# Last bank in pieces of 384 and 128 columns, its last store split by partitions over both hardware queues

## The chip, the cores and the metric

One core of a Trainium2 chip. The metric is the device time of one execution in microseconds (us), of which several are taken; all runs with rounds were in the fast state, with a mean granted TensorE clock of 0.996 to 1.0; the three single looks (e6, e10, e11) are of unknown state. "Before" is the kernel as it was, "the change" the kernel with the diff below.

Since everything happens in the last six microseconds, I use one more measure, the **tail**: from the start of the add of output row block k = 6 (the last instruction chain that the diff leaves alone) to the end of the span. It is read from one profiled execution and does not contain the few tenths by which whole executions differ from one another earlier on.

## The reference

```python
def reference(input, grad_output):          # (16, 512, 1024), (16, 512, 768), float32
    return np.einsum('bmk,bmn->kn', input, grad_output)      # (1024, 768)
```

A matrix product that contracts over 8192 rows, in 64 slices of 128. The kernel rounds the inputs to bf16.

## The kernel before

512 of the 768 output columns are computed in the "wide" form: for each of eight blocks k of 128 output rows, a slice of the input is the weight and 512 columns of grad_output are streamed. Most slices are summed early, in parts, into `acc` in SBUF. The end of the kernel is the last 14 slices (50 to 63) of each of the eight blocks: 14 matmuls into one PSUM bank (where TensorE sums), an add to `acc` on VectorE, a store to HBM (the chip's main memory). Stores are issued by SyncE or by ACT (ScalarE), each with a DMA queue of its own. The last block is cut into three column pieces, so that the last add and the last store are small. Four stores of the other 256 columns (`turned`) stand before that in the program, on the ACT queue; in time the last of them is issued at 162.82 us, just before the store of k = 4.

```python
    rows_of = out.rearrange("(b r) n -> r b n", r=SQ)
    for a in range(P // SQ):
        c = NA + a * NT * SQ
        nc.scalar.dma_start(
            out=rows_of[:, :, c : c + NT * SQ],
            in_=turned[a * SQ : (a + 1) * SQ].rearrange("p b r t -> p b (r t)"),
        )

    for k in range(KS):                                   # KS = 8, NA = 512, NB = 256, P = 128
        slices = range(parts["A" if k < KS // 2 else "B"].done, S)          # 50 .. 63
        pieces = [(0, NA)] if k < KS - 1 else [(0, 256), (256, 384), (384, NA)]
        for c0, c1 in pieces:
            name = free.pop(0)
            bank = psum.tile([P, NA], f32, name=name)[:, 0 : c1 - c0]
            for s in slices:
                wide_mm(bank, k, s, s == slices[0], s == slices[-1], c0, c1)
            add_out(acc[:, k, c0:c1], bank)               # VectorE: acc += bank
            free.append(name)
            W = NB if k < 6 else c1 - c0                  # columns per store
            for c in range(c0, c1, W):
                nc.sync.dma_start(out=OUT[:, k, c : c + W], in_=acc[:, k, c : c + W])
```

## Time and profile before

| | before |
|---|---|
| time, median of the first 3 runs (of the 6 that the change is compared with) | 176.0 us (175.99) |
| span of the profiled execution | 174.3 us |
| TensorE busy | 97% of the span |
| last add ends | 171.79 us into the span |
| last store: issue to landing | 1.54 us |
| last landing to the end of the span ("closing") | 0.92 us |
| tail | 5.86 us |

The prediction shows most of the profile lines on which this rests (in these views DVE is VectorE; SPq and ACTq are the sequencers of SyncE and ACT, which issue the stores). The add of k = 6:

```profile
168.41 0.69 DVE L118 TENSOR_TENSOR acc<-bank,acc 128x512 f32<-128x512 f32 x1 [2.33 <-PE bank L127]
```

The finer times are start times of single records of the trace: an add's start and duration, an issue's start, the last increment of a store's completion semaphore (its "landing"). They read as a relay: matmuls of a piece, add, issue by a queue, bytes in motion, landing, closing. From the last add on nothing else runs beside it, so whatever one link costs the time pays in full.

### The profile page before, as it was taken

How to read it: one execution, taken by the hardware profiler on the slowest of the kernel's cores; microseconds unless marked ns; L12 is line 12 of the kernel's file. 1: busy time of each engine (PE TensorE's matmuls, PEld its weight loads, DVE VectorE, ACT ScalarE, POOL GpSimd, SP SyncE). 2: the span in 40 equal slices, each digit the busy share in tenths (PEclk: the TensorE clock that was granted, in tenths of full speed). 3: DMA queues.
4: the chain of work that ended last, by engine and by line, in shares of the span. 5: the costliest groups of instructions: out<-in, count | busy, mean ns of one | idle time of the engine just before them, and what ended most of it. 6: DMA issues, size and time to landing. Idle time of an engine off the chain costs nothing.

```text
span 174.3 us, 2013 instructions
## 1 busy us (share of the span) xinstructions
PE 169.9 (97%) x793; PEld 78.4 (45%) x808; DVE 61.3 (35%) x103; ACT 6.2 (4%) x12; POOL 66.7 (38%) x129
## 2 busy tenths in 40 slices
PE   8999999999999999999999999999999999999993
PEld 3444444444444444444444444444444444444463
DVE  0655582883940039300000662200560003931122
ACT  2640000000000000000000000000000000000000
POOL 7444434444444444444444444444274200000000
PEclk9999999999999999999999999999999999999999
DMA  5999999999999999999999999999999990085623
GB/s 192 276 208 209 207 209 208 208 208 209 207 208 209 207 208 210 207 209 209 206 209 208 208 210 207 207 209 208 207 209 209 207 202 11 0 190 160 170 86 120
DMA packets 25048, 33.35 MB, mean 191 GB/s; under 512 B 6480, under 2 KB 16592, under 8 KB 25040
## 3 DMA queue, kind: packets, MB, share of 16 engines
q0 software_dynamic: 18000, 28.65, 89.9%
q10 hardware_dynamic: 4448, 2.10, 4.7%
q1 hardware_dynamic: 2592, 2.49, 4.2%
q8 instruction: 6, 0.10, 0.2%
q14 instruction: 2, 0.02, 0.0%
HBM read 58.72 MB, written 3.15 MB: 355 GB/s over the span
## 4 chain that ended last, share of the span: by engine, by line
PE 97%; issue 0%; DVE 0%
PE bank L127 63%; PE bank L134 32%; PE bank L81 3%; DVE acc L118 0%
## 5 line engine op out<-in xcount | busy, mean ns | idle before, releaser
L127 PE MATMUL bank<-gt,xt 128*128 128x512 bf16 (+2 forms) x515 | 108.3, 367 | 0.5
L127 PEld LDWEIGHTS <-xt 128*128 128x128 bf16 x524 | 50.2, 98 | 57.2
L118 DVE TENSOR_TENSOR acc<-bank,acc 128x512 f32<-128x512 f32 (+2 forms) x62 | 37.9, 667 | 73.4 <-PE bank L127 72.9
L134 PE MATMUL bank<-xt,gt 128*128 128x512 bf16 x242 | 54.8, 379 | 0.3
L97 POOL DMA_DIRECT2D xt<-in_input_dram x62 | 33.1, 533 | 38.7 <-DMA xt<-in_input_dram 36.5
L92 POOL DMA_DIRECT2D gt<-in_grad_output_dram x63 | 33.8, 536 | 31.2 <-DMA gt<-in_grad_output_dram 24.9
L134 PEld LDWEIGHTS <-gt 128*128 128x128 bf16 x252 | 24.6, 98 | 29.7
L118 DVE TENSOR_TENSOR acct<-bank,acct 128x512 f32<-128x512 f32 x24 | 15.7, 682 | 30.0 <-PE bank L134 29.9
L81 PE MATMUL bank<-const-bfloat16-1.0 128*128 128x512 bf16 (+1 forms) x12 | 4.6, 574 | 0.8 <-PEq L263 0.8
L81 PEld LDWEIGHTS <-const-bfloat16-1.0 128*128 128x128 bf16 x12 | 1.6, 140 | 3.5 <-issue 3.5
L122 DVE COPY acc<-bank 128x512 f32<-128x512 f32 x4 | 2.7, 687 | 1.0 <-PE bank L127 1.0
L180 DVE STREAM_TRANSPOSE turned<-acct 128x512 f32<-128x512 f32 x4 | 2.9, 715 | 0.1
L127 PEld LDWEIGHTS <-x 128*128 128x128 bf16 x16 | 1.6, 98 | 1.9 <-DVE x L107 0.2
L107 DVE CAST g<-gf 128x256 bf16<-128x256 f32 x2 | 0.6, 290 | 4.7 <-DMA gf<-in_grad_output_dram 4.7
L124 ACT COPY acc<-bank 128x512 f32<-128x512 f32 x4 | 2.1, 589 | 1.3 <-PE bank L127 1.3
L127 PE MATMUL bank<-gt,x 128*128 128x512 bf16 x8 | 2.1, 379 | 0.0
L127 PE MATMUL bank<-g,x 128*128 128x512 bf16 x8 | 2.0, 398 | 0.0
L122 DVE COPY acct<-bank 128x512 f32<-128x512 f32 x2 | 1.3, 686 | 1.3 <-PE bank L134 1.3
L107 ACT CAST x<-xf 128x256 bf16<-128x256 f32 x4 | 1.4, 409 | 0.0
L107 ACT ACT_TABLE_LOAD x1 | 1.3, 1283 | 1.7 <-PEq L263 1.7
L124 ACT COPY acct<-bank 128x512 f32<-128x512 f32 x2 | 1.1, 588 | 1.5 <-PE bank L134 1.5
L107 DVE CAST x<-xf 128x256 bf16<-128x256 f32 (+1 forms) x5 | 1.0, 260 | 0.0
(8 smaller groups left out, 3.3 us busy)
## 6 DMA issues: line engine op xcount, KB each, us to landing
xt<-in_input_dram POOLq DMA_DIRECT2D x62, 256.0 KB, 8.5
gt<-in_grad_output_dram POOLq DMA_DIRECT2D x63, 192.0 KB, 8.5
out_dram<-acc SPq DMA_DIRECT2D x13, 128.0 KB, 2.7
xf<-in_input_dram ACTq DMA_DIRECT2D x2, 512.0 KB, 5.1
out_dram<-turned ACTq DMA_DIRECT2D x4, 256.0 KB, 3.4
gf<-in_grad_output_dram SPq DMA_DIRECT2D x1, 256.0 KB, 3.9
out_dram<-acc SPq DMA_DIRECT2D x1, 256.0 KB, 2.0
gf<-in_grad_output_dram SPq DMA_DIRECT2D x1, 128.0 KB, 4.7
```

The source lines that it names most:

```text
L81: nc.tensor.matmul(wps[:, 0:cols], ones, nc.const_aps.tensor(1.0, (P, cols), bf16), start=True, stop=True,)
L92: nc.gpsimd.dma_start(out=gt, in_=G[s * P : (s + 1) * P, :])
L97: nc.gpsimd.dma_start(out=xs[s], in_=X[s * P : (s + 1) * P, :])
L107: copy(out=dst[:, c0:c1], in_=src[:, c0:c1])
L118: nc.vector.tensor_add(out=dst, in0=src, in1=dst)
L122: nc.vector.tensor_copy(out=dst, in_=src)
L124: nc.scalar.copy(out=dst, in_=src)
L127: nc.tensor.matmul(bank, xs[s][:, k * P : (k + 1) * P], gwide[s][:, c0:c1], start=start, stop=stop)
L134: nc.tensor.matmul(bank, gnarrow[s].rearrange("p (r t) -> p t r", t=NT)[:, t], xs[s][:, h * NA : (h + 1) * NA], start=start, stop=stop,)
L180: nc.vector.transpose(out=turned[:, h * hb : (h + 1) * hb, :, t], in_=dst.rearrange("p (b r) -> p b r", r=SQ),)
```

## The change

Its intent: fewer pieces, so that TensorE ends a little earlier, and the last store in two halves of 64 partitions issued at once by both hardware queues, so that each has half of the rows to issue.

```diff
-        pieces = [(0, NA)] if k < KS - 1 else [(0, 256), (256, 384), (384, NA)]
+        pieces = [(0, NA)] if k < KS - 1 else [(0, 384), (384, NA)]
...
-            W = NB if k < 6 else c1 - c0
+            W = NB if k < KS - 2 else c1 - c0
+            if c1 == NA and k == KS - 1:
+
+                for eng, p0 in ((nc.scalar, 0), (nc.sync, P // 2)):
+                    eng.dma_start(
+                        out=OUT[p0 : p0 + P // 2, k, c0:c1], in_=acc[p0 : p0 + P // 2, k, c0:c1]
+                    )
+                continue
             for c in range(c0, c1, W):
                 nc.sync.dma_start(out=OUT[:, k, c : c + W], in_=acc[:, k, c : c + W])
```

The second hunk is no change of behaviour (KS - 2 is 6).

## The prediction

> **What bounds the kernel now.** I read the page's chain first, then the engine totals, to learn which engine sets the end.
>
> ```profile
> PE 169.9 (97%) x793; PEld 78.4 (45%) x808; DVE 61.3 (35%) x103; ACT 6.2 (4%) x12; POOL 66.7 (38%) x129
> ## 4 chain that ended last, share of the span: by engine, by line
> PE 97%; issue 0%; DVE 0%
> PE bank L127 63%; PE bank L134 32%; PE bank L81 3%; DVE acc L118 0%
> ```
>
> The chain is TensorE's own row of matmuls for 97% of the span. Nothing that the diff touches lies before the last of eight output rows (k = 7), so only the last few microseconds can change. The timeline of that stretch comes next (start, duration, engine, line, operation).
>
> ```profile
> 169.13 3.02 SPq L248 DMA_DIRECT2D out_dram<-acc  x4
> 169.94 0.42 DVE L118 TENSOR_TENSOR acc<-bank,acc 128x256 f32<-128x256 f32 x1 [0.84 <-PE bank L127]
> 170.72 0.29 DVE L118 TENSOR_TENSOR acc<-bank,acc 128x128 f32<-128x128 f32 x1 [0.36 <-PE bank L127]
> 171.50 0.29 DVE L118 TENSOR_TENSOR acc<-bank,acc 128x128 f32<-128x128 f32 x1 [0.49 <-PE bank L127]
> ```
>
> Each add starts when the fourteen matmuls of its piece are done, so the distances between add starts are the lengths of the pieces: k = 6 ended at 168.41 (the add before these in the same view), the 256-column piece took 169.94 - 168.41 = 1.53 us, each 128-column piece 0.78 us. The last add ends at 171.79, and the span at 174.3: 2.5 us with no compute at all. I looked into these with the stretch table (stretch, length, five engines, clock, DMA share, GB/s), cut where DMA activity starts and stops:
>
> ```profile
> 171.20:171.70 0.50, 0.26 (x5) 0.09 (x2) 0.20 (x1) 0.00 (x0) 0.00 (x0) 1.00 0.77 262
> 171.85:172.20 0.35, 0.00 (x0) 0.00 (x0) 0.00 (x0) 0.00 (x0) 0.00 (x0) 1.00 0.64 187
> 172.60:173.00 0.40, 0.00 (x0) 0.00 (x0) 0.00 (x0) 0.00 (x0) 0.00 (x0) 1.00 0.57 164
> 173.00:174.30 1.30, 0.00 (x0) 0.00 (x0) 0.00 (x0) 0.00 (x0) 0.00 (x0) 1.00 0.00 0
> ```
>
> The first three rows are the stores of the 256-, 128- and 128-column pieces (262 x 0.50 = 131 KB; 187 x 0.35 and 164 x 0.40 = 65 KB each). Before and between them the DMA engines are idle. The last store alone reads:
>
> ```profile
> L248 SPq DMA_DIRECT2D out_dram<-acc x1: 333/333/333, 171.8 to 171.8; - x1
> DMA to landing us min/median/max: 1.5/1.5/1.5
> SPq L274 <- DMA out_dram<-acc: 0.7, 1, 0.7
> ```
>
> So the 2.5 us are: add end 171.79 to issue 171.82, 0.03; issue to first byte (172.61), 0.79; bytes in motion until 172.99, 0.38; last byte to landing, about 0.35 (SyncE's wait of the third line ends at 173.37); the program's closing events to 174.27, 0.9. They sum to 2.45.
>
> **What the Trainium skill says.** "TensorE: Matmul & The Clock Gate", section "Back-to-back issue gap", gives N/2.4 + 2.5 ns for an isolated stream and a slower rate where weights are loaded too (81 ns at N = 128). The trace agrees with the first formula: 1.53/14 = 109 ns at 256 columns (formula 109.2), 0.78/14 = 55.7 at 128 (55.8), (168.41 - 165.39)/14 = 215.7 at 512 (215.8). It does not show the 81 ns, although each of these matmuls has its own weight load. "DMA: Bandwidth & Descriptors", section "Rules for kernel authors", says of two transfers to disjoint partition halves "Don't bother", since both halves use the same 16 DMA engines, and that spreading over issuers only saves sequencer issue time. The kernel before has no such pair to show it. "Perfetto Trace Analysis", section "DMA Instruction — HWDGE (DVE, Sync)", says that the descriptor generator is locked by one sequencer at a time. The trace has one overlapping pair of issues, the second ACT store of the transposed part and the first SyncE store:
>
> ```profile
> L230 ACTq DMA_DIRECT2D out_dram<-turned x1: 582/582/582, 152.4 to 152.4; - x1
> L248 SPq DMA_DIRECT2D out_dram<-acc x1: 348/348/348, 152.6 to 152.6; - x1
> ```
>
> ACT's issue ran from about 152.4 for 582 ns, SyncE's from 152.62 for 348 ns: begun inside the other, it took only 16 ns more than the 332 of one alone, and ended first. That speaks against a full wait of one sequencer for the other; but ACT's took 582 against 357 for the store before it, so something was shared.
>
> **The change part by part.**
>
> *Two pieces for three.* It removes one group of fourteen matmuls with their weight loads, one add and one store. Matmul time: before 14 x (109.2 + 55.7 + 55.7) = 3.09 us. A 384-column matmul I interpolate between 256 and 512 columns: (109.2 + 215.7)/2 = 162.5 ns. After: 14 x (162.5 + 55.7) = 3.055 us. TensorE so ends 0.035 us earlier, on the path in full: the last add starts at about 171.465 and ends at 171.755. The smaller count of matmuls frees nothing else, as the last piece stays 128 columns and its add stays 0.29 us.
>
> *The larger store before the last.* Its add starts at 168.41 + 14 x 0.1625 = 170.685 and takes (0.425 + 0.691)/2 = 0.56 us (256 and 512 columns), until 171.245, so it is out of the way of the last add by 0.2 us. SyncE issues the 192 KB at 171.275 and is free again 0.33 later, at 171.605, before the last half needs it at 171.785. First byte 0.82 after issue (169.13 to 169.95 for k = 6, 170.39 to 171.22 for the 256-column piece): 172.10. The 131 KB took 0.48 us in motion, and the 262 KB of k = 6 about 0.75 (169.95 to 170.70), so 192 KB take about 0.61 and end near 172.7. It lands by 173.1, before the last store: not the end itself. But it now overlaps the start of the last store (172.575) by about 0.12 us, where before the engines had 0.4 us of idleness. Its end is thin, as in the other stores, so I charge 0.04 us, at worst 0.1.
>
> *The last store in two halves.* Each half has 64 rows of 512 bytes, four per DMA engine if spread over sixteen; bytes and packets are the same in sum. The 64 KB keep an engine busy for 0.57 x 0.40 = 0.23 us, and the store's 0.38 us in motion are this plus 0.15 us by which the engines start one after another. Two queues can only shorten the 0.15, and the 0.33 us issue if that is proportional to rows. It is not: the row-heavy ACT store (32 partitions x 32 rows of 256 bytes) was issued in 322 ns when alone, the 128-row store in 332. So I expect at most half of the 0.15, and take -0.05 us. The receipt (0.35 us) stays, and the closing (0.9 us) stays; one more queue to wait for costs SyncE a 28 ns event, which it runs while the store is still under way.
>
> *Sum:* -0.035 (TensorE) - 0.05 (split) + 0.04 (overlap with the store ahead) = about -0.05 us, 0.03% of 176.0.
>
> **Rivals.** First, the two issues exclude each other. Then the second half comes 0.25 us (582 - 332) to 0.33 us later; its first byte is at 172.83 to 172.91, and with half the bytes (0.11) plus the 0.15 stagger it ends at 173.09 to 173.17 in place of 172.99: +0.10 to +0.18 in that term, some 176.1 in all. For it: the skill's page and the 582 ns. Against it: SyncE's 348 ns inside the other's issue.
> Second, the halves split the issue and generation work truly, and everything from issue to last byte shrinks: 0.17 us of issue plus 0.08 of stagger, so -0.3 with TensorE, 175.7. For it: engines are only 57% busy in the last store, so it is not bound by bytes. Against it: issue takes 0.33 us whatever the number of rows.
> Third, the 192 KB store blocks the last one for its whole remainder, as it waits ahead of the SyncE half in the same queue: +0.1, with the split void, 176.1. For it: bytes in motion so close together; against it: the k = 6 store moved 347 GB/s with the engines at 0.92, so there is no long queue to drain.
> None of these is near 2% (3.5 us), which is more than the whole stretch from the last add to the end. Only a disturbance outside the change could reach that.
>
> **Range and chances.** Predicted 175.95 us. The three rivals span 175.7 to 176.1; the three runs of before alone span 175.91 to 176.1, and another chip or run may shift both. The range of eight in ten is 175.6 to 176.3. Chances: faster by over 2% 0.005, within 2% 0.99, slower by over 2% 0.005.
>
> **What would show it.** In the changed kernel's trace: fourteen 384-column matmuls, the last two adds' starts 0.78 apart and the last at about 0.035 us earlier than before; the 384-column add at about 0.56 us; the two last issues on ACT and SyncE within 0.05 us of each other, each about 0.33 us (if one is 0.5 or more, the first rival is right; if both are near 0.17, the second); bytes of both stores running into one another between 172.1 and 173.0 with no gap; the last landing near 173.3. The prediction is wrong if the first byte of a half comes much later or earlier than 0.8 us after its issue, or if the receipt of 64 rows differs from that of 128.

## The result and the profile after

The change is **slower by 0.3%**: 176.54 us median (176.37 to 176.88, six runs) against 175.99 (175.78 to 176.47, six runs). The ratio is 1.003, 95% interval 1.0015 to 1.0045. A ratio here is the mean time of one kernel's runs over that of the other's of the same rounds, so not quite the ratio of the medians quoted. By the 2% measure it counts as the same, but the difference is clear of noise, and it lies outside the range that I gave.

The timeline of the changed kernel's end (start, duration, engine, line, operation), against the adds shown in the prediction:

```profile
168.71 0.69 DVE L118 TENSOR_TENSOR acc<-bank,acc 128x512 f32<-128x512 f32 x1 [2.33 <-PE bank L127]
...
170.98 0.56 DVE L118 TENSOR_TENSOR acc<-bank,acc 128x384 f32<-128x384 f32 x1 [1.58 <-PE bank L127]
171.76 0.29 DVE L118 TENSOR_TENSOR acc<-bank,acc 128x128 f32<-128x128 f32 x1 [0.22 <-PE bank L127]
172.09 0.53 SPq L250 DMA_DIRECT2D out_dram<-acc  x1
172.09 0.54 ACTq L250 DMA_DIRECT2D out_dram<-acc  x1
```

First, the add of k = 6 starts at 168.71, where before it started at 168.41. That 0.3 us has nothing to do with the change: the code up to there is the same, and the profiled execution was the slowest of the six (176.88). The medians less the tails agree: 176.54 - 6.39 = 170.15 and 175.99 - 5.86 = 170.13. So I count from this add. To the last add it is now 171.764 - 168.708 = 3.056 us, before 171.501 - 168.410 = 3.091: the pieces gained what was foretold. But the two issues take 0.53 and 0.54 us where the last issue before took 0.33. The issues of this end, one by one (duration minimum/median/maximum in ns, then first and last start in us):

```profile
L255 SPq DMA_DIRECT2D out_dram<-acc x1: 332/332/332, 171.6 to 171.6; - x1
L250 SPq DMA_DIRECT2D out_dram<-acc x1: 530/530/530, 172.1 to 172.1; - x1
L250 ACTq DMA_DIRECT2D out_dram<-acc x1: 543/543/543, 172.1 to 172.1; - x1
```

The stretch table of the changed kernel, cut where DMA activity starts and stops (the last two columns are DMA share and GB/s):

```profile
172.35:173.08 0.73, 0.00 (x0) 0.00 (x0) 0.00 (x0) 0.00 (x0) 0.00 (x0) 1.00 0.75 269
173.25:173.53 0.28, 0.00 (x0) 0.00 (x0) 0.00 (x0) 0.00 (x0) 0.00 (x0) 1.00 0.49 119
173.53:173.85 0.32, 0.00 (x0) 0.00 (x0) 0.00 (x0) 0.00 (x0) 0.00 (x0) 1.00 0.42 101
173.85:175.10 1.25, 0.00 (x0) 0.00 (x0) 0.00 (x0) 0.00 (x0) 0.00 (x0) 1.00 0.00 0
```

The first row is the store of 384 columns (269 x 0.73 = 196 KB). The next two are the halves, some 33 KB each, and the packets' queue numbers say which: SyncE's from 173.26, ACT's from 173.53. Two things strike: the first byte comes 1.17 us after the issue (before 0.83), and the halves do not move together but one after the other, each taking 0.3 us where the whole 64 KB took 0.36. ACT's half lands 2.09 us after its issue, in place of 1.54. The balance of the tail, 6.39 - 5.86 = +0.53 us: TensorE -0.035; issue to landing +0.555; closing 0.918 against 0.917, nothing; the remaining 0.005 in the gap between add and issue. The whole loss lies between the issue of the last store and its landing. A tail comes from one execution of each kernel, but its links repeat between runs: a last store of 128 whole rows behind three pieces lands 1.52 to 1.54 us after its issue (before, e6, e8, e10), ACT's 64-row half 2.09 and 2.10 (the change, e2).

### The profile page after: what moved, and what is told of

It reads as the page before. It is cut to its first block, busy times and chain, and to the rows that moved or that the text cites. A ratio compares the mean times of both kernels' runs of the same rounds, so it can differ in the third digit from the quotient of the medians.

```text
span 175.1 us, 1984 instructions
## 1 busy us (share of the span) xinstructions
PE 170.2 (97%) x779; PEld 77.7 (44%) x794; DVE 61.1 (35%) x102; ACT 6.2 (4%) x12; POOL 66.7 (38%) x129
## 4 chain that ended last, share of the span: by engine, by line
PE 97%; issue 0%; DVE 0%
PE bank L127 63%; PE bank L134 31%; PE bank L81 3%; DVE acc L118 0%
## 5 line engine op out<-in xcount | busy, mean ns | idle before, releaser
L127 PEld LDWEIGHTS <-xt 128*128 128x128 bf16 x510 | 49.4, 98 | 58.0
```

What stands on the lines that cost most here:

```text
L127: nc.tensor.matmul(bank, xs[s][:, k * P : (k + 1) * P], gwide[s][:, c0:c1], start=start, stop=stop)
```

## The experiments

Three theories stood at the start. T1: two sequencers that issue at the same instant hinder each other (the first rival of the prediction, in a stronger form). T2: a store of 64 rows is slow by itself (a later expectation widens this to fewer than 128 rows). T3: the 192 KB store, still in motion until 173.08, holds the last one back. Ratios and medians come with five rounds against the kernel before on the same chip; the three row-count runs are one look each, of unknown state (176.82, 176.31 and 176.69 us; these times are not used), and only single issues, first bytes and closings are read from them.

| run | time, median (before of the same chip) | ratio (95%) | tail | last issue to last landing | closing |
|---|---|---|---|---|---|
| before | | | 5.86 | 1.54 | 0.92 |
| the change | 176.54 (175.99) | 1.003 (1.0015 to 1.0045) | 6.39 | 2.09 | 0.92 |
| e1 pieces only | 176.0 (176.1) | 0.9993 (0.9981 to 1.0005) | 5.91 | 1.57 | 0.97 |
| e2 split only | 177.26 (176.1) | 1.0058 (1.0046 to 1.0071) | 6.86 | 2.10 | 1.35 |
| e3 halves on one queue | 177.02 (176.1) | 1.0047 (1.0035 to 1.0059) | 6.74 | 1.89 | 0.90 |
| e4 whole on ACT | 176.03 (176.1) | 0.9998 (0.9985 to 1.001) | 5.93 | 1.58 | 0.97 |
| e5 halves by columns | 176.13 (176.11) | 1.0004 (0.9992 to 1.0017) | 6.03 | 1.74 | 0.92 |
| e7 pieces, 20 stores | 175.96 (176.11) | 0.9995 (0.9983 to 1.0007) | 5.85 | 1.57 | 0.90 |
| e8 before, 21 stores | 176.58 (176.11) | 1.0034 (1.0022 to 1.0046) | 6.28 | 1.53 | 1.34 |
| e9 96 + 32 rows | 176.29 (176.09) | 1.0007 (0.9992 to 1.0022) | 6.08 | 1.79 | 0.92 |
| e12 wide piece on ACT | 176.2 (176.11) | 1.0016 (1.0 to 1.0032) | 5.96 | 1.60 | 0.98 |

For e3 the "last issue" is the second half's, 0.58 us after the first.

### e1: the pieces alone

```diff
 (from the change)
-            if c1 == NA and k == KS - 1:
-                for eng, p0 in ((nc.scalar, 0), (nc.sync, P // 2)): ...
-                continue
```

> Undoes the split, keeps 384 + 128. Measure of the tail: start of the add of k = 6 to the end of the span, 5.86 us before, 6.39 after. Theory T1 (two sequencers issuing in the same instant hinder each other: 530 and 543 ns instead of 332, and the bytes of the second half only after those of the first): with one issue the loss is gone, the last issue takes 0.33 us, first byte 0.8 us after it, tail 5.8 to 5.9, time within 0.1 us of before (176.0). Rival T3 (the 192 KB store, in motion until 173.08, holds back the last store in its ring): the first byte still comes more than 1.0 us after the issue, tail 6.1 or more, time 176.3 or more.

Measured: no loss. The last issue takes 332 ns, and the store lands 1.571 us after it. T3 falls as the main cause: the 192 KB store is there, and still in motion, yet it delays the last landing by only 1.571 - 1.536 = 0.035 us. The loss is in the split. These 0.035 us use up what TensorE gains (-0.035). That e1's tail is 0.05 us longer than before all the same has a reason of its own (closing 0.97 in place of 0.92), which e7 and e8 find.

### e2: the split alone

```diff
 (from the change)
-        pieces = [(0, NA)] if k < KS - 1 else [(0, 384), (384, NA)]
+        pieces = [(0, NA)] if k < KS - 1 else [(0, 256), (256, 384), (384, NA)]
```

> Keeps 256 + 128 + 128, splits the last store by partitions over both queues; the store ahead is 64 KB and long over. T1: both issues near 0.53 us, halves' bytes one after the other, tail 6.3 to 6.5, time 0.4 to 0.7 us over before. T3: first byte 0.8 us after issue, tail 5.8 to 5.9, no loss.

Measured: issues of 531 and 548 ns, the halves one after the other, 2.10 us from issue to landing, as in the change, although the store ahead of it is 64 KB and long over. That is T1's forecast (and T2's). But the tail is 6.86, above all that T1 allows: the closing takes 1.35 us. Something after the last landing differs too.

### e3: both halves on SyncE, one after the other

```diff
-                for eng, p0 in ((nc.scalar, 0), (nc.sync, P // 2)):
+                for eng, p0 in ((nc.sync, 0), (nc.sync, P // 2)):
```

> 384 + 128, both halves of 64 rows issued one after the other by SyncE. T1: each issue takes 0.33 us, the first half's first byte 0.8 us after its issue, the second half's 0.33 to 0.38 later, tail 6.1 to 6.3 (+0.3 to +0.4 over before). Rival T2 (a store of 64 rows is slow to issue and start by itself): an issue of 0.5 us though alone, first byte at 1.1 or later, tail 6.5 or more. If issue time goes with the number of rows: 0.17 us each and a tail of 5.9.

Measured, the two issues of this run:

```profile
L250 SPq DMA_DIRECT2D out_dram<-acc x1: 528/528/528, 171.7 to 171.7; - x1
L250 SPq DMA_DIRECT2D out_dram<-acc x1: 578/578/578, 172.3 to 172.3; - x1
```

**T1 falls here.** The first half is issued while no other queue issues anything, and it takes 528 ns all the same; its first byte comes 1.17 us after the issue, exactly as beside ACT's. The long issue belongs to the 64-row store, not to the meeting of two queues.

### e4: the last store whole, on ACT

```diff
+                nc.scalar.dma_start(out=OUT[:, k, c0:c1], in_=acc[:, k, c0:c1])
-                (the two halves)
```

> 384 + 128, the last store whole, issued by ACT instead of SyncE. T1: like e1, issue 0.33 us, first byte at 0.8 us, tail 5.8 to 5.9, time within 0.1 us of e1. Rival T4 (ACT's queue starts later by itself): first byte 1.1 us or more after issue, tail 6.1 or more.

Measured: an issue of 357 ns, landing 1.58 us after it, time as e1. A slow ACT queue (T4) is out: 0.01 us of landing at most.

### e5: two halves by columns

```diff
-                for eng, p0 in ((nc.scalar, 0), (nc.sync, P // 2)): ...
+                h = (c0 + c1) // 2
+                nc.scalar.dma_start(out=OUT[:, k, c0:h], in_=acc[:, k, c0:h])
+                nc.sync.dma_start(out=OUT[:, k, h:c1], in_=acc[:, k, h:c1])
```

> T1 has fallen so far as the first half goes: alone on SyncE (the run with both halves on one queue) a 64-row store was issued in 528 ns and had its first byte 1.17 us after the issue, just as beside ACT's. New theory T2: a store of 64 rows costs 0.2 us more of issue and 0.34 us more until its first byte than one of 128 rows, whoever issues it; a second queue adds about 0.2 us of waiting for the later half. Test: the last store in two halves by columns (128 rows of 256 bytes each) at once on ACT and SyncE. T2: issues near 0.33 to 0.36 us, SyncE's first byte at 0.83 us, ACT's some 0.2 to 0.3 later; tail 5.95 to 6.15 us, time 0.1 to 0.3 us over before. Rival (concurrency of two queues lengthens both issues after all, whatever the shape): both issues 0.5 us, tail 6.3 or more.

Measured:

```profile
L250 SPq DMA_DIRECT2D out_dram<-acc x1: 333/333/333, 172.0 to 172.0; - x1
L249 ACTq DMA_DIRECT2D out_dram<-acc x1: 371/371/371, 172.0 to 172.0; - x1
```

Two queues that issue in the same instant, 4 ns apart, take 333 and 371 ns: 1 and 14 more than alone (332 and 357, e1 and e4). SyncE's half lands 1.572 us after its issue, as the whole store in e1; ACT's 1.735 us, that is 0.16 later than a whole store of twice the bytes. So with a harmless shape the split over two queues gains nothing and costs some 0.16 us of landing (0.17 in the tail), too little to be told from zero in the time (interval of the ratio around 1).

### e6, e10, e11: which row counts are slow

```diff
+            cut = {4: 64, 5: 96, 6: 112}.get(k)          # e10: {3: 64, 4: 32, 5: 48, 6: 80}
+            if cut:
+                for p0, p1 in ((0, cut), (cut, P)):
+                    nc.sync.dma_start(out=OUT[p0:p1, k, c0:c1], in_=acc[p0:p1, k, c0:c1])
+                continue
```

> The kernel before, but the stores of k = 4, 5 and 6 (2 KB rows) cut by partitions into 64 + 64, 96 + 32 and 112 + 16, all on SyncE, well before the end; only the durations of issue and the time to the first byte are of interest. If a store of fewer than 128 rows is slow as such: 64, 96 and 112 all near 0.53 us, and the 32 and 16 too. If only certain counts are slow: some stay at 0.33 (a pair's second store at 0.43, as with whole ones back to back). If it was the 512-byte rows together with 64 partitions: 0.33 for all. The end of the program is as before, tail 5.8 to 5.9 us, unless the last store's place in the closing polls shifts (24 - 1 = 23 stores in place of 20: up to +0.4 us).

> One look: the kernel before with the stores of k = 3, 4, 5, 6 cut into 64 + 64, 32 + 96, 48 + 80, 80 + 48 rows on SyncE. The first of a pair is the clean one. T6 (64 alone is slow): 64 near 0.53; 32, 48, 80 near 0.32 to 0.36 (up to 0.45 for the second of a pair). Rival (fewer rows than some limit between 64 and 96 are slow): 32, 48 and 80 or some of them near 0.53 too. The end of the program may be up to 0.4 us later by the place of the last store in the closing polls.

Measured in e6, the first stores of the pairs with 64, 96 and 112 rows:

```profile
L250 SPq DMA_DIRECT2D out_dram<-acc x1: 525/525/525, 163.4 to 163.4; - x1
L250 SPq DMA_DIRECT2D out_dram<-acc x1: 352/352/352, 166.5 to 166.5; - x1
L250 SPq DMA_DIRECT2D out_dram<-acc x1: 317/317/317, 169.5 to 169.5; - x1
```

And in e10 with 64, 32, 48 and 80:

```profile
L250 SPq DMA_DIRECT2D out_dram<-acc x1: 525/525/525, 159.9 to 159.9; - x1
L250 SPq DMA_DIRECT2D out_dram<-acc x1: 350/350/350, 162.9 to 162.9; - x1
L250 SPq DMA_DIRECT2D out_dram<-acc x1: 315/315/315, 165.9 to 165.9; - x1
L250 SPq DMA_DIRECT2D out_dram<-acc x1: 316/316/316, 169.0 to 169.0; - x1
```

T2 stands for 64 rows; its wider form ("fewer than 128 rows are slow as such") falls. Of 32, 48, 64, 80, 96, 112 and 128 rows **only 64 is slow**, by about 0.2 us of issue; the first byte of the 48-, 80-, 96- and 112-row stores comes 0.81 to 0.85 us after the issue, as for 128 rows, and that of the 32-row store 0.86 us after it (the 64-row stores stood beside an ACT store here, so their first byte is not read). 2 KB rows behave like 512-byte ones. The second store of a pair takes 420 to 427 ns for 32, 16, 80, 96 and 48 rows, about the 432 of a whole store issued right behind another; the second 64-row store takes 586. (My count of stores in the expectation of e6 was wrong: it has 21, not 23, and so has e10.)

e11 asks whether it is 64 runs in all or 64 partitions: output blocks k = 3 and 4 stored together as 64 partitions x 2 runs, k = 5 and 6 as 32 x 2 and 96 x 2.

```diff
+            if k in (3, 5):
+                continue
+            cut = {4: 64, 6: 32}.get(k)
+            if cut:
+                for p0, p1 in ((0, cut), (cut, P)):
+                    nc.sync.dma_start(
+                        out=OUT[p0:p1, k - 1 : k + 1, 0:NA], in_=acc[p0:p1, k - 1 : k + 1, :])
+                continue
```

> One look: the kernel before, with output rows k = 3 and 4 stored together after k = 4 in two stores of 64 partitions x 2 runs of 2 KB, and k = 5 and 6 after k = 6 in 32 partitions x 2 runs and 96 partitions x 2 runs. If the 64 partitions matter: the 64 x 2 stores near 0.53, the 32 x 2 near 0.33. If the total of 64 runs matters (four per DMA engine): 32 x 2 near 0.53, 64 x 2 near 0.33. If it is only the flat shape of 64 single runs: both near 0.33.

Measured, the first store of 64 x 2 and that of 32 x 2:

```profile
L252 SPq DMA_DIRECT2D out_dram<-acc x1: 697/697/697, 163.3 to 163.3; - x1
L252 SPq DMA_DIRECT2D out_dram<-acc x1: 345/345/345, 169.3 to 169.3; - x1
```

It goes with a dimension of 64, here the partitions, and not with 64 runs in all: 32 x 2 has these and is issued in 345 ns, while 64 x 2 takes 697, more even than the 0.53 that I expected. Why 64 is a bad count no run tells; I leave it open.

### e9: the same split with 96 and 32 rows

```diff
-                for eng, p0 in ((nc.scalar, 0), (nc.sync, P // 2)): ...
+                for eng, p0, p1 in ((nc.scalar, 96, P), (nc.sync, 0, 96)):
+                    eng.dma_start(out=OUT[p0:p1, k, c0:c1], in_=acc[p0:p1, k, c0:c1])
```

> The change, with its last store cut into 96 rows on SyncE and 32 on ACT in place of 64 and 64. New theory T6, after the row counts (64 rows: 525 ns to issue; 96: 352; 112: 317): it is the count 64, not halving as such, that makes the store slow to issue and start. T6: issues 0.33 to 0.38 us, SyncE's first byte at 0.8 to 0.9 us, only ACT's part later by 0.1 to 0.2 as in the column halves; tail 5.95 to 6.10 us (before 5.86, the change 6.39), time 0.05 to 0.25 us over before. Rival (any cut of the last store by partitions over two queues is slow): issues 0.5 us, tail 6.3 or more, time 0.45 or more over.

Measured, the two issues of this run:

```profile
L249 SPq DMA_DIRECT2D out_dram<-acc x1: 348/348/348, 172.0 to 172.0; - x1
L249 ACTq DMA_DIRECT2D out_dram<-acc x1: 379/379/379, 172.0 to 172.0; - x1
```

Tail 6.08, time 176.29. This is the change with the cut moved from row 64 to row 96 (and ACT given the upper part), and it takes back 0.31 of the 0.53 us of tail. The 0.22 that stay are near the 0.17 of e5, the other split over two queues; I put them down to the second queue, which no further run separates. The saving is read from the traces: the intervals of the two ratios, 0.9992 to 1.0022 here and 1.0015 to 1.0045 for the change, still overlap a little.

### e8 and e7: what the number of stores does to the closing

e2's surplus of 0.43 us after the last landing needed its own explanation. In the records of SyncE's closing the completion semaphores are waited for in a fixed order, one event after the other about 62 ns apart; stores take eight semaphores in rotation. With 20 stores the last one happens to lie on the semaphore waited for last; e2 has 21, and its last store lies on the one waited for first. T5: the seven other waits, long satisfied, then run after the landing.

```diff
 e8, from the kernel before:                     e7, from e1:
-            W = NB if k < 6 else c1 - c0         -            W = NB if k < KS - 2 else c1 - c0
+            W = NB if k < 7 else c1 - c0         +            W = NB if k < KS - 1 else c1 - c0
```

> The kernel before with one harmless change: the store of k = 6 in two of 256 columns, so 21 stores instead of 20. T5 says the last store's semaphore is then the first that SyncE polls at the close, and seven or eight more polls follow the last landing: closing 1.34 us in place of 0.92, tail 6.25 to 6.35, time 0.35 to 0.5 us over before (and this is the 0.42 by which the split-only run was worse than the change itself). Rival: no effect, tail 5.86, time as before.

> The 384 + 128 pieces with the last store whole (e1), and the store of k = 6 in two of 256 columns, so that there are 20 stores as before instead of 19. Theory T5: SyncE's closing polls the completion semaphores in a fixed order, 62 ns each; with 20 stores the last one lies on the semaphore polled last, with 19 on the one before it, which costs one poll. T5: closing (last landing to the end) back from 0.96 to 0.91 us, tail 5.84 to 5.87 against 5.91 in e1, time 0.03 to 0.07 us below e1. Rival (the number of stores does not matter): tail 5.9 as e1.

Measured: e8 is 176.58 against 176.11, ratio 1.0034, by a harmless change at k = 6. Its last store lands 1.53 us after the issue, as before; the closing is 1.34. The waits of SyncE at the close, here e8:

```profile
SPq L274 <- DMA out_dram<-acc: 1.1, 1, 1.1
```

Before it was one wait of 0.7 us (shown in the prediction): SyncE had then got through its other waits before it stood still for the last store. In e8 it stands still at the first wait, for 1.1 us, and does the rest afterwards. Counted from just before the last landing to the end of the span, SyncE's closing events were in the kernel before, and then in e8:

```profile
L274 SPq EVENT_SEMAPHORE  x3: 17/17/28, 173.4 to 174.2; - x3
```

```profile
L274 SPq EVENT_SEMAPHORE  x10: 17/28/28, 173.4 to 174.7; - x10
```

Seven more, for 1.338 - 0.917 = 0.42 us. e6 and e10, with 21 stores too, close in 1.35 each; e11, with 17 stores, has three more waits after its last landing and a closing of 1.10; e1 and e4, with 19, have one and 0.97. e7, the pieces with a twentieth store, goes back to 0.90 and a tail of 5.85. T5 fits every run.

### e12: a try for a version better than both

```diff
 (from e7)
+                eng = nc.scalar if k == KS - 1 and c0 == 0 else nc.sync
-                nc.sync.dma_start(out=OUT[:, k, c : c + W], in_=acc[:, k, c : c + W])
+                eng.dma_start(out=OUT[:, k, c : c + W], in_=acc[:, k, c : c + W])
```

> A try for a version better than both: pieces 384 + 128, 20 stores (k = 6 in two), the last store whole on SyncE, and the 192 KB store ahead of it issued by ACT, so that the last store does not stand behind it in one ring (e1 and the 20-store version landed 0.035 us later after the issue than before). If standing in the same ring was the cost: landing 1.54 us after the last issue, tail 5.80 to 5.83 (before 5.86), time 0.03 to 0.07 us under before, which five rounds may not separate from zero. If the shared DMA engines are the cost, whichever ring: landing 1.57 us or later, tail 5.85 or more, no gain.

Measured: no gain. The last store lands 1.60 us after its issue, later than e7's 1.57, so standing in one queue with the wide store was not the cost. That the shared DMA engines are, as the expectation has it, is what remains and is not shown. And the two last stores got their semaphores in the other order, so one wait followed the landing (closing 0.98). The best version is e7, 175.96 against 176.11, whose interval (0.9983 to 1.0007) does not separate it from before. No version found beats the kernel before.

## Why the prediction was wrong

- **Bound, and where the change can act**: right. Only the relay after k = 6 moved; its 6.39 us against 5.86 is the time's +0.55 within noise.
- **"Two pieces for three", -0.035**: right, 3.056 against 3.091 us. The interpolated 384-column matmul and add (0.557 us) held too.
- **"The larger store before the last", +0.04**: right, +0.035 in e1. Its readings of bytes in motion were some 0.05 to 0.08 us short: the trace has 0.53 and 0.83 us for the 131 and 262 KB stores, and so 0.68 for 192 KB by the same interpolation; it took 0.69.
- **"The last store in two halves", -0.05**: **this is the step that failed.** It measured +0.52 (1.571 us from issue to landing in e1, 2.091 in the change). I reasoned from "issue takes 0.33 us whatever the number of rows", with 32 and 128 partitions as evidence, and did not consider that a count between them could behave differently. With 64 rows the issue takes 0.53 and the first byte comes at 1.17 us. From e5 and e9, about 0.16 to 0.21 us of the 0.52 are the later half of a split over two queues, and the remaining 0.31 to 0.36 go with the count 64. This division rests on differences between runs of slightly different shapes, so it is an estimate, good to some 0.05 us. The prediction's own sign of being wrong, a first byte much later than 0.8 us after its issue, was there; the other, a changed receipt, was not: last byte to landing is 0.35 us in both kernels.
- **The first rival** (issues exclude each other) was the closest in sign, and its mark, "one of the issues 0.5 us or more", did appear. Its mechanism is refuted all the same: a 64-row issue takes 528 ns alone, and two simultaneous issues of 128 rows 333 and 371. A mark that two mechanisms share proves neither. The 582 ns that spoke for it were weak evidence from the start: that ACT store was issued 34 ns after another of its own queue had been issued, and SyncE's stores in that position took 432 to 1348 ns in the kernel before. What is true of it is milder: ACT's half lands about 0.16 us late though its issue is not lengthened.
- **The second rival** (everything shrinks) had no part in it. **The third** (the wide store blocks): 0.035 us in e1, no more.
- **The closing**, "one more queue costs a 28 ns event, while the store is under way": that the closing stays was right for the change, but by luck of its 20 stores (and no event was added: SyncE has 11 in the closing of both kernels); with 21 the same split cost 0.43 us more (e2).
- **Smaller misreadings**: the first byte of the last store before came at 172.65 and not 172.61, so 0.83 us after the issue with 0.36 in motion, not 0.79 and 0.38. The halves have 160 packets together, and not the 144 of the whole store. The bytes of the wide store and of the halves did not run into one another: 0.18 us lay between them.
- **The range**, 175.6 to 176.3, spanned the rivals that I had thought of and missed 176.54 by 0.24.

## What to carry to other kernels

When the last transfer is the end of the program, measure the exact shape before splitting it: here 64 partitions cost 0.2 us of issue, and 0.34 us until the first byte (e3), that the other counts tried did not, and a second queue made the later half later instead of halving the time. Count the stores as well: which completion semaphore the last one gets decided over 0.42 us of waits after its landing, so an edit elsewhere that adds a store can look like a loss of the thing edited. And when a mechanism shows the mark that you foretold, take away its supposed cause once before believing it.

## What the Trainium skill lacked or had wrong

- "DMA: Bandwidth & Descriptors", section "Rules for kernel authors", says of two transfers to disjoint partition halves "Don't bother — they serialize". The trace agrees (SyncE's half in motion from 173.26 to 173.56, ACT's from 173.53 to 173.83), and the prediction left the second clause out. What the row lacks is a loss: the runs show 0.22 us of tail with 96 + 32 rows and 0.53 with 64 + 64.
- No page that I read says that a row count matters to the issue of a store: 525 to 531 ns on SyncE at 64 rows, alone or beside another, against 315 to 352 at 32, 48, 80, 96, 112 and 128.
- "Perfetto Trace Analysis", section "DMA Instruction — HWDGE (DVE, Sync)", has the descriptor generator locked for one sequencer, with the wait inside the reported issue. Two simultaneous issues on SyncE and ACT took 333 and 371 ns, against 332 and 357 alone, so no such wait shows; the second store's landing was later by 0.16 us nevertheless.
- No page that I read mentions the order of the closing waits on the stores' semaphores: about 62 ns each, up to 0.42 us after the last landing.
- "TensorE: Matmul & The Clock Gate", section "Back-to-back issue gap": its formula for an isolated matmul (the prediction says stream) gives 162.5 ns at 384 columns and held here beside weight loads (3.056 us for 14 matmuls of 384 and 14 of 128 columns, formula 3.057). Its rates for a stream with weight loads, 81 ns at 128 columns and 131 at 512, did not show: 55.7 and 215.7 here.
